# Reading the blocks of 128 features at a step of six columns, in a fused LoRA kernel

## Chip, cores, metric

The kernel runs on one core of one Trainium2 chip. The metric is device time in microseconds (us) of one execution.

## The reference

```python
batch, seq, d_model, r = 16, 512, 768, 16      # x: 8192 rows of 768 float32
def reference(x, A, B, scale):                 # A: 768 x 16, B: 16 x 768, scale 0.5
    lora = np.matmul(np.matmul(x, A), B)
    return (x + scale * lora).astype(np.float32)
```

x is 25.2 MB and so is the output. The two matrices are 48 KB each.

## The kernel before

All of x stays in on-chip memory (SBUF), as 128 partitions of 64 rows. Rows are worked on in steps of four. For each step, six blocks of 128 features are transposed on TensorE (four transposes a block), copied to fp16 by ScalarE (ACT), and multiplied by A ("down"); the product is called yt. Then yt is multiplied by B ("up"), VectorE (DVE) adds the result to x in place, and eight rows at a time are stored.

```python
a_f32 = const.tile([P, ND, R], fp32, name="a_f32")                       # P = 128, ND = 6, R = 16
nc.scalar.dma_start(out=a_f32, in_=A.rearrange("(c p) r -> p c r", p=P)) # feature c*128 + p
for n in LOAD_ROWS:                                                      # 1, 3, 4, then 8 seven times
    nc.sync.dma_start(out=x_all[:, ds(r, n), :], in_=xv[:, ds(r, n), :])
    r += n
# ... (cut)
def transposed(r0, S, j):
    xt_ps = ps_xt.tile([P, 4, P], fp32, name="xt_ps")
    for s in range(S):
        nc.tensor.transpose(xt_ps[:, s, :], row(r0 + s)[:, ds(j * P, P)], ident)
    xt_sb = xtpool.tile([P, 4 * P], MM_DT, name="xt_sb")
    nc.scalar.copy(out=xt_sb[:, 0 : S * P], in_=xt_ps[:, 0:S, :])
    return xt_sb
# ... down(): six matmuls, a_mm[:, j, :] stationary, xt moving (cut)
# ... per step: blocks 0-2 transposed, "up" of two rows of the step before, blocks 3-5 transposed,
# ... "up" of its other two rows, then down of this step (cut)
```

In a transpose the data is the stationary operand: the trace has 384 weight loads (LDWEIGHTS, the profile's engine PEld) and 384 multiplications (MATMUL, PE) for the transposes, and when only 64 columns of x are taken (experiment 6) it is the loads that shrink, to 128x64, while the multiplications stay at 128x128. So each of the 384 transposes reads 128 columns of x as weights. And all loads and stores of x are issued on one queue, in that order: the trace has all ten loads issued by 8.2 us and the first store at 27.5 us, so the stores run behind the loads.

## Time and profile before

| | before |
|---|---|
| time, median of runs (lowest to highest) | 125.2 us (125.04 to 125.33) |
| span of the profiled run | 123.6 us |
| DMA queue with x in and out (q1) | 50.33 MB, 96.0% of the span |
| TensorE busy | 80% of the span |
| release of the last store | 107.84 us |
| end of the last DMA packet of x (trace records) | 122.0 us |

The span is what the profiler saw; the timed run is some 1.8 us longer (125.35 us for the one that was profiled). The first lines are from the page of the kernel before: 40 equal slices of the span, each digit the busy share in tenths, then the DMA summary and the small-transfer queue.

```profile
PE   0569997999999999999999999999999995300000
DMA  4999999999999999999999999999999999999981
DMA packets 3416, 50.54 MB, mean 409 GB/s; under 512 B 1088, under 2 KB 1088, under 8 KB 1232
q1 hardware_dynamic: 2592, 50.33, 96.0%
q10 hardware_dynamic: 816, 0.10, 0.6%
```

The DMA engines are busy from the second slice to the end, while PE stops five slices earlier. The DMA stream bounds the kernel. Next, the chain of work that ended last, in the stretch from 40 us on: start, duration, engine, tile and line, count (xt_ps is what the transposes write, lora_ps what "up" writes, yt_ps what "down" writes).

```profile
41.22 1.46 PE xt_ps L82 x12
42.68 0.75 PE lora_ps L108 x4
43.43 1.39 PE yt_ps L92 x6
44.82 1.46 PE xt_ps L82 x12
```

A batch of 12 transposes (L82 is the transpose) takes 1.46 us of TensorE. The single records of the trace show the structure inside it: transposes 109 ns apart; the second weight load of a batch starts 57 ns after the first, later ones 109 ns apart. The next lines are the instructions of that tile (duration in ns: minimum, median, maximum; then first and last start, and shapes counted in a sample of half):

```profile
L82 PEld LDWEIGHTS xt_ps<-ident,x_all x384: 137/140/231, 4.4 to 100.4; 128*128 128x128 f32 x192
L82 PE MATMUL xt_ps<-ident,x_all x384: 272/273/477, 4.5 to 100.5; 128*128 128x128 f32 x192
```

The last two lines show how much room the compute side has: the issue of the last store in the timeline, and how long the SyncE queue (SPq) then waited at the end of the program (L177) for it to land.

```profile
107.84 0.33 SPq L67 DMA_DIRECT2D out_dram<-x_all  x1
SPq L177 <- DMA out_dram<-x_all: 14.3, 1, 14.3
```

The store is released at 107.84 us and lands 14.3 us after that, though one 3 MB store takes about 7.3 us of the stream (estimated from 3.15 MB and the 424 to 433 GB/s that the trace shows from 30 to 110 us). So it waits about 6 us behind earlier stores. The chain of waits gives PE 75% of the span, but it runs through a store that then stands in a queue; PE is not the bound.

### The profile page before, as it was taken

The page shows a single profiled execution, that of the slowest core. Times are in us where ns is not written, and L with a number is a line of the kernel's source. Part 1 is how long each engine was busy: PE and PEld are TensorE (multiplying, and loading weights), DVE is VectorE, ACT ScalarE, POOL GpSimd, SP SyncE. Part 2 cuts the span into 40 slices and gives each one's busy share as a digit, 9 for nine tenths or more (in the row PEclk, how much of TensorE's full clock was granted, in tenths as well). Part 3 has the DMA queues.
Part 4 walks back from the last instruction along what each step waited for, and adds up shares of the span by engine and source line. Part 5 has one row for each costly group of instructions (what it writes and reads, how often), then busy time and mean ns, then how long its engine had stood idle before and what let it go on. Part 6 is the DMA issues. An engine that isn't in the chain of part 4 may idle for free.

```text
span 123.6 us, 1623 instructions
## 1 busy us (share of the span) xinstructions
PE 98.4 (80%) x614; PEld 60.9 (49%) x614; DVE 68.7 (56%) x83; ACT 52.4 (42%) x103; POOL 0.7 (1%) x6
## 2 busy tenths in 40 slices
PE   0569997999999999999999999999999995300000
PEld 0356472847575666666665747475656662000000
DVE  0023156666857677686868686867576688900000
ACT  4315363547373737365555546373737360000000
POOL 2000000000000000000000000000000000000000
PEclk9999999999999999999999999999999999855555
DMA  4999999999999999999999999999999999999981
GB/s 72 383 409 442 477 414 398 485 379 453 430 390 496 398 411 453 406 469 406 406 475 392 446 422 430 453 406 435 430 422 461 392 453 427 414 469 398 446 366 48
DMA packets 3416, 50.54 MB, mean 409 GB/s; under 512 B 1088, under 2 KB 1088, under 8 KB 1232
## 3 DMA queue, kind: packets, MB, share of 16 engines
q1 hardware_dynamic: 2592, 50.33, 96.0%
q10 hardware_dynamic: 816, 0.10, 0.6%
q8 instruction: 5, 0.08, 0.3%
q14 instruction: 3, 0.02, 0.0%
HBM read 25.26 MB, written 25.17 MB: 408 GB/s over the span
## 4 chain that ended last, share of the span: by engine, by line
PE 75%; DMA 5%; DVE 4%; issue 1%; DVEq 1%; SPq 0%
PE xt_ps L82 39%; PE lora_ps L108 19%; PE yt_ps L92 17%; DMA x_all<-in_x_dram 5%; DVE x_all L112 3%; DVE yt_sb L96 1%; DVEq L177 1%; SPq L60 0%
## 5 line engine op out<-in xcount | busy, mean ns | idle before, releaser
L112 DVE TENSOR_TENSOR x_all<-x_all,lora_ps 128x768 f32<-128x768 f32 x64 | 58.3, 951 | 28.7 <-PE lora_ps L108 28.7
L84 ACT CAST xt_sb<-xt_ps 128x512 f16<-128x512 f32 (+2 forms) x102 | 51.2, 568 | 47.3 <-PE xt_ps L82 47.1
L82 PE MATMUL xt_ps<-ident,x_all 128*128 128x128 f32 x384 | 52.0, 287 | 5.6 <-DMA x_all<-in_x_dram 5.6
L82 PEld LDWEIGHTS xt_ps<-ident,x_all 128*128 128x128 f32 x384 | 43.4, 145 | 17.9 <-issue 10.6
L108 PE MATMUL lora_ps<-b_mm,yt_sb 16*128 16x512 f16 (+1 forms) x128 | 27.0, 326 | 2.7 <-DVE yt_sb L96 1.6
L92 PE MATMUL yt_ps<-xt_sb,a_mm 128*16 128x512 f16 (+2 forms) x102 | 24.8, 384 | 0.0
L108 PEld LDWEIGHTS <-yt_sb 16*128 16x128 f16 x128 | 9.4, 93 | 13.8 <-issue 6.8
L92 PEld LDWEIGHTS <-a_mm 128*16 128x16 f16 x102 | 8.0, 93 | 13.6 <-issue 6.0
L96 DVE TENSOR_SCALAR yt_sb<-yt_ps 16x512 f16<-16x512 f32 (+2 forms) x17 | 10.9, 641 | 3.6 <-PE yt_ps L92 3.6
L72 DVE CAST a_mm<-a_f_77 128x96 f16<-128x96 f32 x1 | 0.2, 209 | 4.7 <-DMA a_f_77<-in_A_dram 4.7
L84 ACT ACT_TABLE_LOAD x1 | 1.3, 1283 | 1.8 <-issue 1.8
L74 DVE CAST b_mm<-b_f_89 16x768 f16<-16x768 f32 x1 | 0.5, 548 | 2.1 <-DMA b_f_89<-in_B_dram 2.1
masks.py:199 POOL TENSOR_SCALAR_AFFINE_SELECT ident<-ident 128x128 f32<-128x128 f32 x1 | 0.3, 292 | 0.1
masks.py:197 POOL MEMSET ident<- 128x128 f32 x1 | 0.2, 204 | 0.3 <-POOLq L163 0.3
L163 POOL MEMSET const-bfloat16-1.0<- 128x1 bf16 x1 | 0.1, 102 | 0.0
L163 POOL MEMSET const-uint8-127<- 128x1 uint8 x1 | 0.1, 102 | 0.0
L163 POOL MEMSET const-float32-0.0<- 128x1 f32 x1 | 0.1, 98 | 0.2 <-issue 0.2
L163 POOL MEMSET const-float32-1.0<- 128x1 f32 x1 | 0.1, 98 | 0.0
## 6 DMA issues: line engine op xcount, KB each, us to landing
out_dram<-x_all SPq DMA_DIRECT2D x8, 3072.0 KB, 28.6
x_all<-in_x_dram SPq DMA_DIRECT2D x7, 3072.0 KB, 37.5
x_all<-in_x_dram SPq DMA_DIRECT2D x1, 1536.0 KB, 10.0
x_all<-in_x_dram SPq DMA_DIRECT2D x1, 1152.0 KB, 6.7
x_all<-in_x_dram SPq DMA_DIRECT2D x1, 384.0 KB, 3.6
a_f_77<-in_A_dram ACTq DMA_DIRECT2D x1, 48.0 KB, 3.9
b_f_89<-in_B_dram ACTq DMA_DIRECT2D x1, 48.0 KB, 5.8
```

Source lines behind the costliest of these rows:

```text
L72: nc.vector.tensor_copy(out=a_mm, in_=a_f32)
L74: nc.vector.tensor_copy(out=b_mm, in_=b_f32)
L82: nc.tensor.transpose(xt_ps[:, s, :], row(r0 + s)[:, ds(j * P, P)], ident)
L84: nc.scalar.copy(out=xt_sb[:, 0 : S * P], in_=xt_ps[:, 0:S, :])
L92: nc.tensor.matmul(yt_ps[:, 0:n], a_mm[:, j, :], xt[:, 0:n], start=(j == 0), stop=(j == ND - 1))
L96: nc.vector.tensor_scalar(out=yt_sb[:, 0:n], in0=yt_ps[:, 0:n], scalar1=sc, scalar2=None, op0=mybir.AluOpType.mult,)
L108: nc.tensor.matmul(lora_ps[:, ds(n0, n)], yt_sb[:, ds(s * P, P)], b_mm[:, ds(n0, n)], start=True, stop=True,)
L112: nc.vector.tensor_tensor(out=row(r0 + s), in0=row(r0 + s), in1=lora_ps, op=mybir.AluOpType.add)
L163: nc = _bacc.Bacc("TRN2", target_bir_lowering=False, num_devices=1)
L177: with _tile.TileContext(nc) as tc:
```

## The change

The intent: contiguous, larger packets for A. Feature p*6 + c instead of c*128 + p goes to partition p, so that a partition's 96 numbers of A are 384 consecutive bytes. For the product to stay right, block j of x must then be the columns j, j+6, j+12, ... instead of 128 consecutive ones. The result is correct either way.

```diff
-    nc.scalar.dma_start(out=a_f32, in_=A.rearrange("(c p) r -> p c r", p=P))
+    nc.scalar.dma_start(out=a_f32, in_=A.rearrange("(p c) r -> p c r", p=P))
...
-            nc.tensor.transpose(xt_ps[:, s, :], row(r0 + s)[:, ds(j * P, P)], ident)
+            nc.tensor.transpose(xt_ps[:, s, :], row(r0 + s).rearrange("p (k c) -> p c k", c=ND)[:, j, :], ident)
```

## The prediction

> **What bounds the kernel now.** The DMA stream. The page's slices show the 16 DMA engines at nine tenths from slice 2 to the end; queue q1 takes 96.0% of the span and moves 50.33 MB at about 430 GB/s (windows by stage). All ten loads are issued in the first 8.2 us on the queue that also has the stores, so the stores run behind the loads: the packet records show loads until about 61 us, then stores until 122.0 us, each 3 MB store about 7.3 us. TensorE is busy 80% but ends at 106.6 us; the last store is released at 107.9 us (timeline), while its packets start near 114.5 us. So compute may end some 6 us later before the DMA stream has a hole. The chain of waits names PE for 75%, but it passes through a store that then waits in the queue.
>
> **What the change does.**
> 1. A's load: today about 800 small packets of 11 ns median, 8.8 us in all, 0.55 us for each of 16 engines, beside the first loads of x. With 128 packets of 384 B I estimate 0.15 us: at most 0.4 us off the DMA stream. A's landing is not on the compute path: a_mm is ready at 4.9 us, first used at 6.09 us.
> 2. All other counts and sizes stay.
> 3. Each of the 384 transposes loads x as weights (the stationary operand) with a step of 24 bytes instead of 4. This is the risk. [...] This trace has no such weight load, so the penalty's size is not shown.
>
> **Cost of step 3.** Warm, the records give one transpose per 109 ns inside a batch of 12; the second weight load of a batch starts 55 ns after the first, later ones 109 ns apart. I read this as: reading contiguous weights takes 55 ns and hides behind a 109 ns matmul; only a batch's first load is bare. Estimates:
> - No penalty: nothing changes.
> - Half the rate (most likely): 110 ns a load, just hidden; transposes 109 to 113 ns apart, plus 55 ns bare for each of about 34 batches. Compute ends about 3 us later, inside the slack. Time unchanged or 0.3 us lower.
> - A quarter: about 215 ns a load, which then sets the pace. 350 warm transposes x 106 ns plus 34 x 160 ns is about 43 us; the last store is released near 151 us, about 11 us of store and tail follow: about 163 us. DMA would no longer bound it.
> - In between (160 ns): about 140 us.
>
> **Prediction.** 125.0 us, range 124.2 to 141. Faster by over 2%: 0.02; within 2%: 0.64; slower by over 2%: 0.34.
>
> **What would show it.** Queue q10 down from 816 packets to about 176, its share from 0.6% to 0.2%. Weight loads of the transposes longer than 140 ns, and their spacing in a batch: at 109 to 113 ns I am right; clearly above, wrong. The last store's release: up to 114 us harmless. DMA at nine tenths to the end if the stream still binds; holes in the last third if compute does. DVE additions (951 ns) and ACT copies (594 ns) unchanged.
>
> **What would make it wrong.** A strided weight load slower than half rate; strided and moving reads disturbing each other so that loads no longer hide; the profile's durations for weight loads being a model, so that 55 ns isn't the reading time.

The 125.0 us are the 125.2 us measured before, less a part of the 0.3 us that A's load might save, with nothing added for compute that ends about 3 us later, since about 6 us of slack were read from the trace. "Warm" means the later part of the trace, where transposes come 109 ns apart. The 55 ns come from the trace; half the rate, a quarter and 160 ns are assumptions, and that half was the most likely one, and the odds with it, was not shown by anything. The 0.15 us for A's new packets is an estimate given without its working.

## The result

The changed kernel took 130.72 us (median of 4; 130.04 to 130.83) beside 125.18 us for the kernel before: ratio 1.0431, 95% interval 1.0394 to 1.0469. It is slower. Ratios in this document are the mean time of one kernel's fast runs over that of the other's fast runs of the same rounds, so they are not quite the ratios of the medians quoted. The time lies in the predicted range, but the class that I held most likely ("within 2%") was the wrong one.

The page of the changed kernel, the same lines:

```profile
PE   0589997999999999999999999999999999972000
DMA  4999999999999999999999999999999973980892
DMA packets 2776, 50.54 MB, mean 392 GB/s; under 512 B 448, under 2 KB 448, under 8 KB 592
q1 hardware_dynamic: 2592, 50.33, 92.1%
q10 hardware_dynamic: 176, 0.10, 0.2%
```

The saving is there: 640 small packets fewer in q10. By the packet records, 768 packets of 64 B (11 ns each in the median) became 128 of 384 B (22 ns), and q10 without B's packets of 3 KB went from 8.8 to 3.1 us, 0.55 to 0.20 us for each of 16 engines. But PE now works two slices longer (of slightly longer slices), and the DMA row has holes near the end: slices with 7, 3, 8, 0. The stream ran out of released stores. The chain, the tile and the last store of the changed kernel:

```profile
42.25 1.83 PE xt_ps L82 x12
44.08 0.75 PE lora_ps L108 x4
44.83 1.82 PE xt_ps L82 x12
46.65 0.75 PE lora_ps L108 x4
47.40 1.39 PE yt_ps L92 x6
```

```profile
L82 PEld LDWEIGHTS xt_ps<-ident,x_all x384: 209/239/243, 4.6 to 111.7; 128*128 128x128 f32 x192
L82 PE MATMUL xt_ps<-ident,x_all x384: 273/300/503, 4.7 to 111.8; 128*128 128x128 f32 x192
119.15 0.33 SPq L67 DMA_DIRECT2D out_dram<-x_all  x1
SPq L177 <- DMA out_dram<-x_all: 8.3, 1, 8.3
```

A batch of transposes takes 1.83 us instead of 1.46; the other batches on PE (0.75 and 1.39 us) have not moved. The weight loads are 239 ns long instead of 140 (medians), and single transposes are 133 to 137 ns apart instead of 109. The last store is released at 119.15 us, 11.3 us later than before, and then lands in 8.3 us: nothing stands before it in the queue any more. The sum fits. 29 batches that ran at full clock in both kernels cost 0.365 us more each, 10.6 us. (In the records, the first two transposes of a batch went from 164 to 238 ns apart, the others from 109 to between 133 and 139.) One more batch, near 15 us, took 2.40 instead of 1.53 us: the trace's first record of full clock comes at 16.65 us here and at 15.18 us in the kernel before. Against that stand 0.2 us of an earlier start. That makes 11.3 us of later compute, of which the queue hid 5.9; the DMA stream ended 5.45 us later (127.47 against 122.02) and the time grew by 5.5.

One observation in the trace needs no experiment. At the start transposes are 213 ns apart in *both* kernels. I call this half clock: no clock record covers it, but in every trace the pace falls from 213 ns within 0.8 us of the first record of full clock, which came between 12.2 and 29.8 us. What raises the clock, the runs don't show. The changed kernel's first load of a batch takes about 210 ns there and also later at full clock; the kernel before has 181 to 183 ns at half and 138 ns at full clock. So the strided load did not get faster with the clock, and where the matmul beside it is long enough it costs next to nothing (0.03 us a batch of nine).

### The profile page after: what moved, and what is told of

Its sections match the earlier page's. It is cut to its first block, busy times and chain, and to the rows that moved or that the text cites. A ratio compares the mean times of both kernels' runs of the same rounds, so it can differ in the third digit from the quotient of the medians.

```text
span 128.9 us, 1623 instructions
## 1 busy us (share of the span) xinstructions
PE 110.0 (85%) x614; PEld 74.0 (57%) x614; DVE 68.8 (53%) x83; ACT 55.8 (43%) x103; POOL 0.7 (1%) x6
## 3 DMA queue, kind: packets, MB, share of 16 engines
q1 hardware_dynamic: 2592, 50.33, 92.1%
## 4 chain that ended last, share of the span: by engine, by line
PE 81%; DMA 5%; DVE 4%; issue 1%; DVEq 1%; SPq 0%
PE xt_ps L82 46%; PE lora_ps L108 18%; PE yt_ps L92 17%; DMA x_all<-in_x_dram 5%; DVE x_all L112 3%; DVE yt_sb L96 1%; DVEq L177 1%; SPq L60 0%
## 5 line engine op out<-in xcount | busy, mean ns | idle before, releaser
L84 ACT CAST xt_sb<-xt_ps 128x512 f16<-128x512 f32 (+2 forms) x102 | 54.6, 561 | 55.3 <-PE xt_ps L82 55.3
L82 PE MATMUL xt_ps<-ident,x_all 128*128 128x128 f32 x384 | 63.6, 318 | 5.3 <-DMA x_all<-in_x_dram 5.3
L82 PEld LDWEIGHTS xt_ps<-ident,x_all 128*128 128x128 f32 x384 | 56.5, 236 | 17.6 <-PE yt_ps L92 7.1
```

Source lines behind the costliest of these rows:

```text
L82: nc.tensor.transpose(xt_ps[:, s, :], row(r0 + s).rearrange("p (k c) -> p c k", c=ND)[:, j, :], ident)
```

## The experiments

My theory after the result was: (1) the strided weight read alone costs the time, A's load gives nothing back; (2) weights for the next transpose are loaded while the present one runs, so a transpose costs the longer of the 109 ns matmul and the load; (3) the store queue hides the first 5.9 us. Rivals: the new load of A disturbs the start; strided reads slow the matmul beside them; the time grows with each slow transpose, with no slack at all.

### 1 and 2: each half of the change alone

Both give a wrong result, since A and the blocks of x no longer match. Edit of `e1_a_only`: only the first pair of lines of the diff above. Edit of `e2_stride_only`: only the second pair.

> Only A's load changed (128 packets of 384 B), transposes contiguous as before; result wrong on purpose, since A's rows no longer match the features. Theory (the strided weight read costs the time): 124.8 to 125.3 us, transposes 109 ns apart, q10 at 176 packets. Rival (the new load of A, or its place among the first loads, costs the time): 130 to 131 us.

> Only the transposes changed (step of 24 bytes), A loaded as before in 768 packets; result wrong on purpose. Theory: 130.5 to 131.2 us, transposes 133 to 137 ns apart, weight loads 239 ns. Rival (A's load is the cause): 125.2 us.

| | time, us | ratio to before (95%) | transposes apart | last store released |
|---|---|---|---|---|
| `e1_a_only` | 125.47 | 1.0016 (0.9987 to 1.0046) | 109 ns | 108.10 us |
| `e2_stride_only` | 130.55 | 1.0437 (1.0397 to 1.0477) | 133 to 137 ns | 118.97 us |

A batch of the chain and the last store of `e2_stride_only`:

```profile
55.08 1.83 PE xt_ps L82 x12
118.97 0.33 SPq L67 DMA_DIRECT2D out_dram<-x_all  x1
```

The strided read alone brings the whole growth. `e1_a_only` lies just above the 124.8 to 125.3 us that I expected, and far below the rival's 130. A's new load brings no gain that five rounds can see: the 0.4 us that I had costed at most would be 0.997, below the whole interval, and the measured middle lies on the other side of 1. Where the freed DMA time went, no run shows. In the changed kernel the second load of x did land a little earlier (its first transposes start at 7.78 instead of 8.03 us), but that is compute time, of which the kernel before has slack.

### 3 and 4: is there slack, and how much?

`e3_half_rows` uses the strided transposes for rows 0 to 31 only; both layouts of A are loaded. The result is right.

```diff
+    nc.scalar.dma_start(out=a2_f32, in_=A.rearrange("(p c) r -> p c r", p=P))   # just after a_f32
-            nc.tensor.transpose(xt_ps[:, s, :], row(r0 + s)[:, ds(j * P, P)], ident)
+            nc.tensor.transpose(xt_ps[:, s, :], (<strided> if r0 < HALF else <contiguous>), ident)   # HALF = 32
-            prev = (r0, S, down(xts, S))
+            prev = (r0, S, down(xts, S, a2_mm if r0 < HALF else a_mm))
```

> Rows 0 to 31 with the strided transposes, rows 32 to 63 contiguous; both layouts of A loaded; result right. The changed kernel's compute ended 11.3 us later and its time grew by 5.5 us, so I think about 5.8 us are hidden by the store queue. Theory (slack): half the strided transposes move the end of compute by about 5.7 us, nearly all hidden: 125.0 to 126.0 us. Rival (no slack; the time grows with each slow transpose, the small growth having another cause): half of the growth, about 127.9 us.

It took 127.83 us (ratio 1.0210, 1.0172 to 1.0249; "unclear" at the 2% mark), just what the rival had said. The trace shows why that doesn't speak for the rival. The chain of waits of this run begins with:

```profile
1.23 9.07 DMA a_f<-in_A_dram
10.32 0.22 DVE a_mm L77
10.54 0.04 issue
10.59 0.81 PE yt_ps L97 x6
```

The second load of A landed only at 10.3 us and held back the first matmul on it, so compute started late: the last store was released at 116.38 us, not near the 113.5 us that I had meant to test. After that release it landed in 8.3 us, exactly as in the changed kernel. The test was spoiled by my own addition, but its end still follows a rule: *the stream ends at the later of about 122 us and the last release plus 8.3 us*.

`e11_late_rows` tests that rule with less of the fault: only rows 40 to 63 are strided, the second A is loaded after B, and its conversion is written where row 16 is reached. The result is right. (The edit, against e3; the matching choice of A in "down" is cut in both.)

```diff
+    nc.scalar.dma_start(out=a2_f32, in_=A.rearrange("(p c) r -> p c r", p=P))   # now after B
+        if r0 == 16:
+            nc.vector.tensor_copy(out=a2_mm, in_=a2_f32)
-            ... if r0 < HALF else ...
+            ... if r0 >= LATE else ...                                           # LATE = 40
```

> The half-rows run failed as a test: its second load of A landed at 10.3 us and held the first matmul on A back by over 4 us. Here only rows 40 to 63 are strided and the second A is loaded after B and first used late; result right. Rule from the runs so far: the end is the later of 122.0 us and the last store's release plus 8.3 us. 24 rows x 6 transposes x 26.5 ns plus about 12 bare first loads x 50 ns is 4.4 us: release near 112.3 us, under 113.7 us, so 125.2 to 125.6 us. Rival (time grows with each slow transpose): 24/64 of 5.5 us, about 127.3 us.

It took 125.50 us (ratio 1.0026, 1.0003 to 1.0050) where the rival wanted 127.3. The release came at 113.50 us, 1.2 us later than I had worked out, and still under 113.7. The fault had not quite gone: in this run's trace the conversion of the second A (L140) ran at 11.0 us, long before row 16, and VectorE stood 3.5 us waiting for it to land; the next "up" started 1.3 us late for that reason. The rule needs only the release, so it is tested all the same. So 5.7 us of later compute cost some 0.3 us.

```profile
L140 DVE CAST a_mm<-a_f 128x96 f16<-128x96 f32 x1 | 0.2, 210 | 3.5 <-DMA a_f<-in_A_dram 3.5
113.50 0.33 SPq L69 DMA_DIRECT2D out_dram<-x_all  x1
```

In all six kernels whose release came at 113.70 us or later, the last packet landed 8.27 to 8.34 us after it. In the other eight the stream ended between 121.4 and 122.8 us, so the rule's 122 is good to some 0.8 us (e11: 122.84). The pairs of lines are the last store's issue and the wait for it, for the step of 16 bytes (experiment 5) and for e3:

```profile
113.70 0.33 SPq L67 DMA_DIRECT2D out_dram<-x_all  x1
SPq L177 <- DMA out_dram<-x_all: 8.3, 1, 8.3
```

```profile
116.38 0.33 SPq L70 DMA_DIRECT2D out_dram<-x_all  x1
SPq L182 <- DMA out_dram<-x_all: 8.3, 1, 8.3
```

A release at 113.70 us is the very edge: 113.70 + 8.3 = 122.0, and that kernel took 125.25 us. Beyond it, each microsecond of later compute was a microsecond of time: e3's 2.7 us cost 2.6, the changed kernel's 5.45 cost 5.5.

### 5: what the step of the read costs

Here the step changes (and, for 8 and 12 bytes, A's load with it); the transposes, their number and their 128 columns stay. Steps of 8 and 12 bytes can be made right with blocks of 256 and 384 columns (A's packets are then 128 and 192 bytes). Steps of 16, 48 and 96 bytes read the wrong columns; 48 and 96 bytes run across two and four rows of x, in steps of four rows. Theory A is: between steps 8 and 24 at 12 bytes, and the same as step 24 at 16 and 96 bytes; the two earlier rules that the text for 48 bytes calls fallen are A and B. The first numbers for 8 bytes are those of contiguous columns.

```diff
-            nc.tensor.transpose(xt_ps[:, s, :], row(r0 + s)[:, ds(j * P, P)], ident)
+ 8, 12 B:   row(r0 + s).rearrange("p (g k c) -> p g c k", k=P, c=CS)[:, j // CS, j % CS, :]     # CS = 2, 3
+ 16 B:      row(r0 + s)[:, j * 40 : j * 40 + 509 : 4]
+ 48 B:      x_all[:, r0 + s - s % 2 : r0 + s - s % 2 + 2, :].rearrange("p s (k c) -> p (s k) c", c=12)[:, :, 2 * j + s % 2]
+ 96 B:      x_all[:, r0 : r0 + 4, :].rearrange("p s (k c) -> p (s k) c", c=24)[:, :, j * 4 + s]
```

> Blocks of 256 columns, every second column of each: step of 8 bytes[...]; A's packets 128 B, 384 of them; result right. [...] transposes 109 ns apart, weight loads 140 ns, second load of a batch 55 to 57 ns after the first, 124.9 to 125.3 us. Rival (any step other than 4 bytes halves the read): pace 133 to 137 ns and about 130.7 us.

> Step of 12 bytes (blocks of 384 columns, every third)[...]; result right. Step 8 gave 96 ns from first to second load and 120 ns a transpose, step 24 gave 107 and 135. Theory A [...]: between the two, about 100 ns and 125 to 130 ns, 125.2 to 127.5 us. Theory B (any step over 4 bytes costs one fixed rate[...]): 96 ns and 120 ns as with step 8, 125.2 to 125.7 us.

> Step of 16 bytes[...]; result wrong on purpose (columns read twice). Theory A [...]: same as step 24, 107 ns from first to second load, 133 to 137 ns a transpose, about 130.5 us. Theory B (distance): less than step 24, 96 to 102 ns and about 120 to 128 ns.

> Step of 96 bytes across the four rows of a step; result wrong on purpose. Theory A [...]: nothing beyond step 24 bytes: 107 ns, 133 to 137 ns a transpose, about 130.5 us. Theory B (distance matters further): slower, over 110 ns from first to second load and over 140 ns a transpose, over 132 us.

> Step of 48 bytes across two rows of x; result wrong on purpose. Both earlier rules [...] fell: transposes were 120 ns apart at 8 bytes, 114 at 12, 120 at 16, 135 at 24, 111 at 96, and the pace follows the length of the weight read. Open is whether 24 bytes is one slow step or one of a family. Theory C (multiples of 24 bytes that are not multiples of 16 are the slow ones, 48 is a multiple of 16): 109 to 121 ns a transpose, 124.8 to 125.6 us. Theory D (the read is slowest for steps of some 24 to 48 bytes and gets faster beyond): 125 to 137 ns and 127 to 131 us.

All numbers but the time are read from the single records of the trace at full clock: the median duration of a batch's first weight load (which runs beside no transpose), and the median distance of transposes, a batch's first pair left out.

| kernel | step, bytes | first load, ns | transposes apart, ns | pace less first load | last release, us | time, us |
|---|---|---|---|---|---|---|
| before | 4 | 138 | 109 | hidden | 107.84 | 125.2 |
| `e4_step2` | 8 | 195.5 | 120 | -75.5 | 112.75 | 125.56, ratio 1.0026 (0.9996 to 1.0056) |
| `e5_step3` | 12 | 192 | 114 | -78 | 111.01 | 124.82, ratio 0.9981 (0.9962 to 0.9999) |
| `e6_step4` | 16 | 196 | 120 | -76 | 113.70 | 125.25 (one run) |
| after | 24 | 211 | 136 | -75 | 119.15 | 130.72 |
| `e12_step12` | 48 | 202 | 127 | -75 | 114.85 | 126.48 (one run) |
| `e7_step24` | 96 | 186 | 111 | -75 | 109.42 | 124.78 (one run) |

Three things follow. First, every step tried above 4 bytes lengthens the first load, from 138 ns to between 186 and 211 ns, also the step of 8 bytes (195.5 ns): my expectation for `e4_step2` failed on the pace (120 ns, not 109) and the time came out a little above it (125.56 us, 124.9 to 125.3 expected); it stayed that near because its release at 112.75 us is still inside the slack. Second, the cost is not the same for all steps from 16 bytes on (16, 24, 48 and 96 bytes gave 120, 136, 127 and 111 ns a transpose; 8 bytes costs as much as 16), and it does not grow with distance (96 bytes is the cheapest). Theories A and B of these expectations both fall (B had the numbers for 16 bytes right, 97 ns from first to second load and 120 ns a transpose, but not those for 96), and so does C; of D, the pace fits and the time was just under its range. Twenty-four bytes, the step of this change, is the slowest of the six strided ones tried. What makes it so I can't say: the runs show the dependence, not its cause. The place where a block starts is not it: the changed kernel's blocks start 0 to 20 bytes into a row, and its transposes stayed 133 to 139 ns apart. Third, in all six the pace is the first load's duration less 75 to 78 ns. I read that constant as the part of a load that overlaps with its neighbours; the rest sets the pace once it is over 109 ns. Experiment 6 finds the same split in another way.

The step of 12 bytes is the fastest correct kernel run here, by 0.2% (about 0.3 us) with an interval that nearly reaches 1. I would not call that a gain worth having.

### 6: does the load hide behind the matmul, or slow it?

The identity still moves 128 columns, so the matmul stays at 109 ns, but only M columns of each block are taken as weights. Features are left out, so the result is wrong.

```diff
-            nc.tensor.transpose(xt_ps[:, s, :], <128 columns>, ident)
+            nc.tensor.transpose(xt_ps[0:M, s, :], <first M of them>, ident)      # copy and down on 0:M as well
```

> Each transpose takes only 64 contiguous columns as weights, the identity still moves 128 columns; result wrong on purpose (half the features left out). Control: both theories say 109 ns a transpose, about 125.2 us; the second load of a batch about 28 to 30 ns after the first.

> The same 64 columns at a step of 24 bytes; wrong on purpose. Theory (the next weights are loaded while a matmul runs; a transpose costs the longer of the 109 ns matmul and the load plus some 27 ns): load 54 ns, so 109 ns a transpose, fully hidden, about 125.2 us. Rival (strided reads slow the matmul beside them: the surplus of 26 ns for 128 elements halves with the elements): about 122 ns a transpose, about 126 us.

> 96 columns at a step of 24 bytes; wrong on purpose. Theory (longer of 109 ns and load plus 27 ns): load 80 ns, so 107 ns: still hidden or just at the edge, 109 to 111 ns a transpose. Rival (surplus in proportion to the elements): 128 to 129 ns a transpose.

The tile's lines for 64 contiguous, 64 strided and 96 strided columns, one kernel a fence; under the strided ones, batches from the chain (the one at 14.46 us is at half clock):

```profile
L83 PEld LDWEIGHTS xt_ps<-ident,x_all x384: 108/111/177, 4.1 to 101.4; 128*64 128x64 f32 x192
```

```profile
L83 PEld LDWEIGHTS xt_ps<-ident,x_all x384: 142/144/178, 4.3 to 106.5; 128*64 128x64 f32 x192
L83 PE MATMUL xt_ps<-ident,x_all x384: 272/273/438, 4.3 to 106.6; 128*64 128x128 f32 x192
14.46 2.72 PE xt_ps L83 x12
68.27 1.47 PE xt_ps L83 x12
```

```profile
L83 PEld LDWEIGHTS xt_ps<-ident,x_all x384: 176/178/208, 4.7 to 100.2; 128*96 128x96 f32 x192
L83 PE MATMUL xt_ps<-ident,x_all x384: 272/273/468, 4.8 to 100.3; 128*96 128x128 f32 x192
67.32 1.50 PE xt_ps L83 x12
```

In all three, transposes are 109 ns apart at full clock (medians of the records), although the last two read at 24 bytes. Their chains say the same: a batch of 12 took 1.46 to 1.47 us with 64 strided columns, 1.50 with 96. A strided read beside it did not slow the matmul; the rival (122 and 128 ns) falls. The times, 125.16, 125.56 and 125.43 us, are single looks. The 64 strided columns were released at 114.01 us for another reason: in that run the transposes were 213 ns apart, the pace of half clock, until about 29 us.

These runs also correct my own picture. The first load of a batch lasts 144, 178 and 211 ns (medians of the records) for 64, 96 and 128 columns at 24 bytes: 1.05 ns for each column, (211 - 144) / 64. Contiguous, 109 and 138 ns give 0.45 ns a column. So I estimate 128 x 1.05 = 134 ns of reading for the strided load of 128 columns, and that meets the pace of 133 to 137 ns with nothing added; the remaining 77 of the 211 ns are the constant of experiment 5. I had read the 107 ns between the first two loads of a batch as the reading time, and needed "some 27 ns" of hand-over to reach 135. Those starts give the same cost for a column (40 ns for 64, 107 for 128: 1.05) but stand some 27 ns lower, and pace less this distance is not the same for every step (20 ns at 12 bytes, 26 at 48). So I take 107 ns for too short a reading of the load; at 24 bytes alone the pace can't tell the two pictures apart. For 96 columns the reading is 101 ns by the same estimate, under 109, which is why it hides.

## Why the prediction was right or wrong

- *The DMA stream bounds the kernel.* Right for before. The change ended that: q1 fell from 96.0% to 92.1% of the span, with holes near the end.
- *Compute may end some 6 us later before the stream has a hole.* Right: 5.9 us (122.0 less 8.3 less 107.84), borne out by the releases at 112.75, 113.50 and 113.70 us that cost next to nothing and those at 116.38 and 119.15 that cost all their excess.
- *A's load: packets from 816 to about 176, share 0.6% to 0.2%.* Right to the packet. *"At most 0.4 us off the DMA stream", "unchanged or 0.3 us lower"*: no gain was measured for it (1.0016, interval 0.9987 to 1.0046).
- *The weight read is the risk, and its load would show as longer than 140 ns.* Right: 239 ns, and the strided read alone gives the whole growth.
- *"Half the rate (most likely): 110 ns a load, just hidden; transposes 109 to 113 ns apart".* This is the step that failed. (The bare read of contiguous weights, 55 ns in the prediction, is 57 in the records, which matters little.) The mechanism, a load that hides until it is longer than the matmul, is what the runs show: at 24 bytes, 96 columns (101 ns of reading, estimated above) came 109 ns apart, 128 columns (134 ns) 133 to 137. The mis-sized term is the load: 134 ns of reading (1.05 ns a column against 0.45, so about 0.43 of the rate), hence 133 to 137 ns a transpose. The 109 ns of the matmul left no room for that: at half the rate the load would just have fitted (110 ns, the prediction's estimate of twice 55), at 0.43 it overhung by some 26 ns for eleven of a batch's twelve transposes, and the first, bare one cost 74 ns more: 0.365 us for each of the 29 batches. Half the rate was an assumption: no trace had shown a strided load. The prediction had listed "a strided weight load slower than half rate" as the first thing that would make it wrong, and its own sum, fed with 134 ns, gives about 130.3 us (350 x 25 ns and 34 x 79 ns after 107.9 us, then 11 us).
- *"Compute ends about 3 us later, inside the slack".* It follows from that term: 11.3 us later, 5.4 us beyond the slack.
- *Additions and copies unchanged.* The additions are at 951 ns as before; the copies of 512 columns went from 594 to 586 ns, which matters to nothing.

The range held because the case of an even slower load was in it, and not because 134 ns had been foreseen; the odds were on the wrong side.

## What to carry to other kernels

In this kernel a stationary operand that is read with a step made a transpose slower than the same transpose of contiguous columns (120, 114 and 136 ns apart at 8, 12 and 24 bytes instead of 109), although the result and every count of instructions stayed the same: before trading a strided read in the inner loop for a better one-time load, compare how often each happens (384 times against once here). Here a load that hid behind a matmul was free only up to the matmul's own length (109 ns), so read both from the trace, and measure the load by varying its width and not by the distance of two starts. And before costing a slower engine, find how long the last output waits in its queue: here 5.9 us of slower compute were free and the rest was not.
